# The store of one expert as four DMAs of 112, 10, 5 and 1 rows

## The chip, the cores and the metric

The kernel runs on one core of a Trainium2 chip. The metric is the device time of one execution in microseconds (us), as the median of several runs. One execution was also recorded by the hardware profiler; the lines shown in this document come from its trace.

Of the core's engines, TensorE (PE, and PEld for its weight loads) multiplies, VectorE (DVE) and ScalarE (ACT) move results out of PSUM and transpose, GpSimd (POOL) issues the loads of the weights, and SyncE (SP) issues the stores and hands out releases. The core has 16 DMA engines, which all queues share. A DMA that has landed adds 16 to its semaphore, one for each of these engines.

## The reference

Eight experts, each a two-layer network on its own 256 rows, in float32:

```python
n_experts, capacity, hidden, expert_hidden = 8, 256, 512, 2048
h = np.matmul(x, w1) + b1[:, np.newaxis, :]
h = np.maximum(h, 0)
return (np.matmul(h, w2) + b2[:, np.newaxis, :]).astype(np.float32)
```

The weights are 4 MB each for w1 and w2 of one expert, 64 MB together. The output is 8 x 256 x 512 float32, 4 MB, or 512 KB for one expert.

## The kernel before

The work is laid out in steps `s`. In step `s` TensorE computes the first layer of expert `s` and then the second layer of expert `s - 3` (LAG = 3). So the last three steps have a second layer alone: experts 5, 6 and 7. The first layer is 16 column blocks of 128 with four matmuls each; ScalarE adds the bias, applies relu and writes float16. The second layer has two row blocks `tb` of 128 rows and 16 contractions `j` each. It runs in a loop of two turns of 14 matmuls, and four matmuls behind them. Before each of the two turns TensorE waits for one release (`s_go`), which it takes off the semaphore at the turn's end.

Weights come in order on POOL's queue, converted to float16 on the way: w1 of the later experts, then w2. The w2 of the last two experts are cut, so that their parts can be released one by one: expert 6 in two halves, expert 7 in a half and two quarters.

When a second layer is done, ScalarE evicts the first row block from PSUM and VectorE the second (the copies at line 196). Results of experts 0 to 3 gather in one tile and of experts 4 and 5 in another; those of 6 and 7 have a tile each.

SP's program is one list, written out by hand (lines 249 to 276). For each step it waits for the weights (line 236) and gives the release (line 237). For the last step it reads:

```python
go(f"w2_{e}_0")
nc.sync.wait_ge(landed[f"w2_{e}_{second}"], 16)
for first in GROUPS:
    flush(first)
for tb in range(nTB):
    nc.sync.wait_ge(s_out[tb], e)
store(E - 2, 0, P, nc.sync)
go(f"w2_{e}_{third}")
```

The order is thus: the release for the first turn of expert 7; the stores of experts 0 to 3 (2 MB) and of 4 and 5 (1 MB), issued at line 241, as soon as the second part of w2 of expert 7 is there; the wait for the eviction of expert 6 (line 271); the store of expert 6 (line 247); the release for the second turn of expert 7, once the last quarter of its weights has landed. Behind that stand the waits for the eviction of expert 7 (line 275) and its store (line 247 again). SP executes this list strictly in order: what stands behind an instruction that takes long, waits with it.

In the 128-row store of one expert, a row is one SBUF partition: two rows of the output, 4 KB. In the two gathered stores a partition has 16 KB and 8 KB.

All stores add to one semaphore, `s_last`. At the start it is raised by 16 for each store and lowered again behind the waits for the first data; an instruction of ScalarE at the kernel's end waits for 16 times the number of stores. For that the code counts the stores: `STORES = len(LATE) + len(GROUPS)`, which is 4.

Of the kernel before, what the change touches and what calls it, by code (L numbers as in the profile page):

```python
# [10 lines left out]
def kernel(  # L11
# [12 lines left out]
    nc = tc.nc  # L24
# [4 lines left out]
    E, T, H = x.shape  # L29
    M = w1.shape[2]  # L30
    P = 128
# [8 lines left out]
    NW = 3  # L40
    NPH = 4
    GROUPS = {0: 4, 4: 2}
    LATE = (E - 2, E - 1)
    CUTS = {E - 2: (0, half, nJ), E - 1: (0, half, half + half // 2, nJ)}
    X_LOADS = {2: 2, 4: 4}
    group_of = {first + i: (first, n) for first, n in GROUPS.items() for i in range(n)}
# [5 lines left out]
    def sem(name):  # L52
        return ctx.enter_context(nc.semaphore(name=name))
# [45 lines left out]


    s_last = sem("last_stores")
    STORES = len(LATE) + len(GROUPS)
    nc.vector.sem_inc(s_last, 16 * STORES)


# [71 lines left out]
    tc.wait_critical_data_deps()  # L177
    nc.vector.sem_inc(s_last, -16 * STORES)
    nc.vector.sem_inc(s_xT, 1)
# [55 lines left out]
    def go(key, n=1):  # L235
        nc.sync.wait_ge(landed[key], 16)  # L236
        nc.sync.sem_inc(s_go, n)  # L237

    def flush(first):
        n = GROUPS[first]  # L240
        nc.sync.dma_start(
            out=out[first : first + n].rearrange("e (p r) h -> (e p) r h", r=n * nTB),
            in_=results[first][:]).then_inc(s_last, 16)

    def store(e, p0, p1, engine):
        dst = out[e].rearrange("(p r) h -> p r h", r=nTB)
        engine.dma_start(out=dst[p0:p1], in_=results[e][p0:p1]).then_inc(s_last, 16)

    for s in range(E + LAG):
        if s == 0:  # L250
            nc.sync.wait_ge(landed["b2"], 16)
        if s < E:
            nc.sync.wait_ge(s_xT, s + 1)
            go(f"w1_{s}")
        e = s - LAG
        if e >= 2:
            for tb in range(nTB):
                nc.sync.wait_ge(s_out[tb], e - 1)
        if e >= 0 and e not in CUTS:
            go(f"w2_{e}_0", 2)  # L260
        elif e == E - 2:
            go(f"w2_{e}_0")
            go(f"w2_{e}_{half}")
        elif e == E - 1:
            _, second, third, _ = CUTS[e]
# [3 lines that stand above are left out]
                flush(first)  # L269
            for tb in range(nTB):  # L270
                nc.sync.wait_ge(s_out[tb], e)
            store(E - 2, 0, P, nc.sync)
            go(f"w2_{e}_{third}")
    for tb in range(nTB):
        nc.sync.wait_ge(s_out[tb], E)
# [62 lines left out]
    section.close()  # L338
    landing = nc.scalar.nop().wait_op(s_last, 16 * STORES, "sem-ge")
    tc.add_manual_dep(landing.ins, by_hand.name, mybir.DependencyInfo(  # L340
# [31 lines left out]
```

## Time and profile before

| What | us |
|---|---|
| median of the runs (180.67 to 180.83) | 180.68 |
| the profiled execution | 180.71 |
| its span, first to last instruction | 178.9 |
| TensorE busy | 134.0 |
| ScalarE busy | 75.6 |
| VectorE busy | 65.0 |
| POOL busy | 12.4 |

The mean granted clock of TensorE is 0.976 of the full one. The span is 1.8 us shorter than the execution, since the start and the end of the program lie around it. A row of the timeline gives start, duration, engine, line, operation and what it writes and reads; in brackets stands the idle time of the engine before it and what ended that. `SPq` is an instruction that SP's sequencer carries out, such as issuing a DMA: its duration is the time in which SP can do nothing else, and has nothing to do with how long the data take. The time "to landing" goes from the start of the issue to the last of its 16 counts.

### The profile page before, as it was taken

What the parts mean: (1) busy time and instruction counts of PE and PEld (TensorE: products, weight loads), DVE (VectorE), ACT (ScalarE), POOL (GpSimd) and SP (SyncE); (2) the same over time, 40 slices, a digit from 0 to 9 for tenths busy, and PEclk for the clock granted to TensorE, in tenths of its full rate; (3) what the DMA queues carried; (4) which work ended last, traced back from release to release, by engine and by line L of the source; (5) the groups of instructions that cost most, each with busy time, mean ns of one, the idle gap of its engine ahead of it and who ended that gap; (6) DMA issues with size and microseconds to landing.
All of it is one profiled execution on the core that took longest, in us unless ns stands there. A gap on an engine that the chain in (4) does not pass through costs nothing. (4 is left out here: it accounts for less than half of the span.)

```text
span 178.9 us, 2980 instructions
## 1 busy us (share of the span) xinstructions
PE 134.0 (75%) x784; PEld 93.0 (52%) x784; DVE 65.0 (36%) x92; ACT 75.6 (42%) x153; POOL 12.4 (7%) x26
## 2 busy tenths in 40 slices
PE   0003978868699890998968896989698896999960
PEld 0003878858689330894458543874298442433420
DVE  1989928475000289600097006910330003031010
ACT  3201786757777113582087505680387201021010
POOL 4300012020200101001010001000200003000000
PEclk9999999999999999699999999699999999999997
DMA  6999999999998999999999999899999999999996
GB/s 218 266 205 207 234 205 205 234 216 196 236 223 185 236 227 194 223 231 201 212 234 209 201 234 223 190 231 231 194 220 231 205 209 211 216 216 207 355 414 256
DMA packets 3970, 40.46 MB, mean 226 GB/s; under 512 B 464, under 2 KB 480, under 8 KB 1408
## 3 DMA queue, kind: packets, MB, share of 16 engines
q0 software_dynamic: 3056, 35.14, 92.7%
q1 hardware_dynamic: 864, 5.24, 7.2%
q10 hardware_dynamic: 48, 0.07, 0.1%
q14 instruction: 2, 0.02, 0.0%
HBM read 71.39 MB, written 4.19 MB: 422 GB/s over the span
## 5 line engine op out<-in xcount | busy, mean ns | idle before, releaser
L297 PE MATMUL ph<-xT,w_sb 128*128 x512 | 72.5, 303 | 33.0 <-PEq L282 30.5
L297 PEld LDWEIGHTS ph<-xT,w_sb 128*128 x512 | 66.6, 146 | 39.9 <-issue 31.4
L224 ACT ACTIVATE hT<-ph,b1T 128x256 f16<-128x256 f32 x128 | 60.2, 475 | 33.4 <-PE ph L297 29.9
L314 PE MATMUL po<-w_sb,hT 128*128 x256 | 56.7, 379 | 2.2 <-issue 2.2
L120 DVE STREAM_TRANSPOSE xT<-x 32x256 f16<-32x256 f16 (+2 forms) x64 | 45.0, 702 | 27.3 <-DMA x<-in_x_dram 22.7
L314 PEld LDWEIGHTS po<-w_sb,hT 128*128 x256 | 24.9, 97 | 33.0 <-issue 7.0
L196 DVE COPY out<-po 32x512 f32<-32x512 f32 (+1 forms) x20 | 13.7, 687 | 63.1 <-PE po L314 62.9
L196 ACT COPY out<-po 32x512 f32<-32x512 f32 (+1 forms) x20 | 11.6, 578 | 46.0 <-PE po L314 45.8
L89 POOL DMA_DIRECT2D w_sb<-in_w_dram x19 | 10.7, 567 | 136.9 <-PE po L314 71.7
L324 PE MATMUL po<-b_sb,ones 1*128 x16 | 4.8, 378 | 3.9 <-issue 2.5
L196 ACT COPY x<-po 128x512 f32<-128x512 f32 x2 | 1.2, 586 | 14.2 <-PE po L314 14.2
L196 DVE COPY x<-po 128x512 f32<-128x512 f32 x2 | 1.4, 692 | 13.9 <-PE po L314 13.9
L324 PEld LDWEIGHTS po<-b_sb,ones 1*128 1x128 f16 x16 | 1.4, 90 | 6.6 <-issue 6.3
L181 DVE STREAM_TRANSPOSE b1T<-b_rows 32x512 f32<-32x512 f32 x4 | 4.1, 1024 | 0.5 <-issue 0.5
L135 ACT CAST x<-x 128x1024 f16<-128x1024 f32 x1 | 1.0, 1046 | 3.2 <-DMA x<-in_x_dram 3.2
L133 DVE CAST x<-x 128x1024 f16<-128x1024 f32 x1 | 0.7, 694 | 2.9 <-DMA x<-in_x_dram 2.9
L127 ACT ACT_TABLE_LOAD x1 | 1.3, 1283 | 0.7 <-PEq L356 0.7
L89 POOL DMA_DIRECT2D x<-in_x_dram x2 | 1.1, 544 | 0.0
L89 POOL DMA_DIRECT2D b_sb<-in_b_dram x1 | 0.5, 509 | 0.0
L126 DVE MEMSET ones<- 1x128 f16 x1 | 0.2, 165 | 0.9 <-PEq L356 0.9
L127 ACT ACTIVATE warm<-ones 1x128 f16<-1x128 f16 x1 | 0.3, 308 | 0.0
L356 POOL MEMSET const-float32-0.0<- 128x1 f32 x1 | 0.1, 99 | 0.2 <-issue 0.2
(3 smaller groups left out, 0.3 us busy)
## 6 DMA issues: line engine op xcount, KB each, us to landing
w_sb<-in_w_dram POOLq DMA_DIRECT2D x14, 2048.0 KB, 41.1
w_sb<-in_w_dram POOLq DMA_DIRECT2D x3, 1024.0 KB, 25.0
out_dram<-out SPq DMA_DIRECT2D x1, 2048.0 KB, 7.3
x<-in_x_dram SPq DMA_DIRECT2D x2, 512.0 KB, 3.8
x<-in_x_dram POOLq DMA_DIRECT2D x1, 1024.0 KB, 34.3
w_sb<-in_w_dram POOLq DMA_DIRECT2D x2, 512.0 KB, 18.2
out_dram<-out SPq DMA_DIRECT2D x1, 1024.0 KB, 9.4
out_dram<-x SPq DMA_DIRECT2D x2, 512.0 KB, 7.2
```

Source lines behind the costliest of these rows:

```text
L89: engine.dma_start(**kw).then_inc(landed[key], 16)
L120: last = nc.vector.transpose(out=mine[b * B : (b + 1) * B].rearrange("p kc (r g i) -> p g r kc i", r=R, i=B)[:, g], in_=src[:, :, b * (H / ...
L126: nc.vector.memset(ones1[:], 1.0)
L127: tc.keep_in_program_order(nc.scalar.activation(out=warm[:], in_=ones1[:], func=relu).then_inc(s_first, 1))
L133: nc.vector.tensor_copy(out=x16[0][0][:], in_=x32[0][:])
L135: tc.keep_in_program_order(nc.scalar.copy(out=x16[1][0][:], in_=x32[1][:]))
L181: turned = nc.vector.transpose(out=b1T[b * B : (b + 1) * B, nB - 1 - b : nB - 1 - b + nJ * B], in_=b1_rows[:].rearrange("r (i j) -> r j i" ...
L196: last = copy(out=results[e][at : at + rows, tb * n + k, :], in_=po[k * rows : (k + 1) * rows, bank : bank + H])
L224: nc.scalar.activation(out=dst, in_=src, func=relu, bias=b1T[:, bias_at : bias_at + 1], scale=1.0,).then_inc(s_credit, 1)
L297: last = nc.tensor.matmul(ph[:, j % NPH, 0:T], w1_sb[:, bass.ds(w_from + (kc * M + j), P, nJ)], xT[:, bass.ds(x_at + kc * T, T)], start=(k ...
L314: return nc.tensor.matmul(banks[tb], hT[:, bass.ds(h_from + (j * nTB + tb) * P, P)], w2_sb[:, bass.ds(w2_from + j * H, H)], start=False, s ...
L324: nc.tensor.matmul(banks[tb], ones1[:], b2_sb[:, bass.ds(s * H, H)], start=True, stop=False)
```

## The change

The store of expert 6, one DMA of 128 partitions, becomes four DMAs of 112, 10, 5 and 1 partitions. They stand at the same place of SP's list, behind the wait for the eviction of expert 6 and ahead of the release for the second turn of expert 7. The bytes are the same. The number of stores that the last wait counts rises from 4 to 7 (`len(DEAL)` is 5: four parts of expert 6 and the store of expert 7).

```diff
     GROUPS = {0: 4, 4: 2}
-    LATE = (E - 2, E - 1)
...
-    STORES = len(LATE) + len(GROUPS)
+    DEAL = (0, 112, 122, 127, 128)
+    STORES = len(GROUPS) + len(DEAL)
...
             for tb in range(nTB):
                 nc.sync.wait_ge(s_out[tb], e)
-            store(E - 2, 0, P, nc.sync)
+            for p0, p1 in zip(DEAL, DEAL[1:]):
+                store(E - 2, p0, p1, nc.sync)
             go(f"w2_{e}_{third}")
```

## The prediction

> **What bounds the kernel now.** I read the page's slices and chain first, then the DMA queues, then the last 15 us.
>
> ```profile
> span 178.9 us, 2980 instructions
> ...
> GB/s 218 266 205 207 234 205 205 234 216 196 236 223 185 236 227 194 223 231 201 212 234 209 201 234 223 190 231 231 194 220 231 205 209 211 216 216 207 355 414 256
> ...
> q0 software_dynamic: 3056, 35.14, 92.7%
> q1 hardware_dynamic: 864, 5.24, 7.2%
> ...
> DMA 22%; PE 22%; issue 2%; DVE 0%; ACT 0%; SPq 0%
> ...
> out_dram<-out SPq DMA_DIRECT2D x1, 2048.0 KB, 7.3
> ...
> out_dram<-out SPq DMA_DIRECT2D x1, 1024.0 KB, 9.4
> out_dram<-x SPq DMA_DIRECT2D x2, 512.0 KB, 7.2
> ```
>
> The weight loads on queue q0 fill the 16 DMA engines until about 166 us; in the last slices SP's queue q1 drains all 4 MB of output. The whole change lies in this tail. The busy time in stretches of it (columns: stretch, its length, then PE, PEld, DVE, ACT, POOL; granted clock, DMA share, GB/s):
>
> ```profile
> 166.00:168.00 2.00, 2.00 (x10) 0.97 (x10) 0.00 (x0) 0.00 (x0) 0.00 (x0) 1.00 1.13 311
> 168.00:170.00 2.00, 2.00 (x10) 0.87 (x9) 0.00 (x0) 0.00 (x0) 0.00 (x0) 1.00 1.01 434
> 170.00:172.00 2.00, 2.00 (x11) 0.89 (x10) 0.00 (x0) 0.00 (x0) 0.00 (x0) 1.00 1.01 434
> 172.00:174.00 2.00, 1.01 (x5) 0.27 (x3) 0.69 (x1) 0.59 (x1) 0.00 (x0) 1.00 0.92 389
> 174.00:176.00 2.00, 0.00 (x0) 0.00 (x0) 0.00 (x0) 0.00 (x0) 0.00 (x0) 1.00 0.98 406
> ```
>
> From 168 us the engines store at 434 GB/s, 27.1 GB/s each, without a gap. TensorE finishes at 173.0, DMA only at the end. The timeline of SP, TensorE and VectorE, start and duration in us:
>
> ```profile
> 157.88 7.08 PE L314 MATMUL po<-w_sb,hT 128*128 x32 [0.26 <-issue]
> 165.76 0.82 SPq L241 DMA_DIRECT2D out_dram<-out  x2
> 165.88 7.13 PE L314 MATMUL po<-w_sb,hT 128*128 x32 [0.30 <-issue]
> 166.69 1.74 SPq L247 DMA_DIRECT2D out_dram<-x  x1
> 168.94 0.10 PEld L314 LDWEIGHTS po<-w_sb,hT 128*128 x1 [0.37 <-issue]
> 173.04 0.69 DVE L196 COPY x<-po 128x512 f32<-128x512 f32 x1 [7.36 <-PE po L314]
> 173.83 0.33 SPq L247 DMA_DIRECT2D out_dram<-x  x1
> ```
>
> The reader is to see that the 512 KB store of expert 6 holds SP 1.74 us, and that the second half of expert 7's matmuls sits behind it: SP's next instruction is the release for that half, at 168.5 (the last start in the L237 row below). TensorE just feels it: the weight load at 168.94 has a gap of 0.37 us.
>
> ```profile
> L237 SPq EVENT_SEMAPHORE  x18: 17/28/9606, 15.4 to 168.5; - x18
> ...
> L241 SPq DMA_DIRECT2D out_dram<-out x2: 348/387/426, 165.8 to 166.2; - x2
> L247 SPq DMA_DIRECT2D out_dram<-x x2: 333/1036/1740, 166.7 to 173.8; - x2
> ...
> DMA to landing us min/median/max: 4.2/8.4/10.1
> ```
>
> So the last store, issued at 173.83, lands 4.2 us later, 178.03. From there to the end of the span are 0.87 us. The profiled execution's own time is 180.71, 1.81 over its span and 0.03 over the median of the runs, 180.68.
>
> **Why the issue takes 1.74 us.** Four issues of stores have the same form; three took 333, 348 and 426 ns. What was different? Packets that began in a stretch, by queue:
>
> ```profile
> q0 software_dynamic: 79, 0.32, 104.7%
> issues: line engine op xcount, KB each, median us to landing
> out_dram<-out SPq DMA_DIRECT2D x1, 2048.0 KB, 7.3
> out_dram<-out SPq DMA_DIRECT2D x1, 1024.0 KB, 9.4
> out_dram<-x SPq DMA_DIRECT2D x1, 512.0 KB, 10.1
> ...
> q1 hardware_dynamic: 16, 0.26, 100.6%
> q0 software_dynamic: 22, 0.03, 26.2%
> ```
>
> The first five lines are 165.76 to 167.27: all three stores are issued, yet only weights move. The last two are 167.27 to 167.89: 16 packets of q1, 16 KB each, the first row of the 2 MB store on each of the 16 engines. The held issue ends at 166.69 + 1.74 = 168.43, 0.54 after the slowest engine turned to q1. When the last store is issued at 173.83, the 2 MB store has landed (165.76 + 7.3 = 173.1) and the 1 MB store is under way, and the issue takes 333 ns. Both fit one reading: two stores of this queue may stand that have not begun on every engine, and a third issue holds SP until the older of the two has begun everywhere. That is inferred from one hold.
>
> **The change, part by part.** Removed: one issue of 128 rows. Added: issues of 112, 10, 5 and 1 rows in its place, same waits ahead, same bytes, and three more counted completions. Behind them on SP stand the release for the second half of expert 7, the waits for its eviction, and the last store. POOL's queue issues nothing more by then.
>
> (1) *112 rows.* It meets the same two stores ahead: 1.74 us, until 168.43. No change.
>
> (2) *10 rows.* Lower bound, an unhindered issue, 0.33 us. Upper: until the 1 MB store has begun everywhere. The 2 MB ahead of it take 2.097 MB / 434 GB/s = 4.83 us from 167.89, so 172.72, and with the lag of 0.54 the issue ends at 173.26. I take the upper one: its nearest row is the 1740 ns one, with two unbegun stores ahead as here, not the 333 ns one.
>
> (3) *5 rows.* Lower bound 0.33 again. Upper: until the 112 rows have begun: 1.049 MB / 434 = 2.42 us more, 175.14, and 0.54: 175.68. Taken for the same reason.
>
> (4) *1 row.* Between 0.33 and the 1.06 us that 112 rows take (0.459 MB / 434) with the lag of 0.54 once more. I take 0.39, the mean of the two unhindered issues at L241, since the ten rows stand on fewer engines: 176.07. The release follows at 176.1 instead of 168.5: 7.6 us later. TensorE has nothing else: its queue goes on only after that release, so all 7.6 reach the last matmul, 173.02 + 7.6 = 180.6.
>
> (5) *The clock.* A TensorE that stood idle came back at half clock:
>
> ```profile
> 71.84 3.36 PE L297 MATMUL ph<-xT,w_sb 128*128 x17 [4.95 <-PEq L282]
> ```
>
> ```profile
> 88.25:91.66 3.41, 1.88 (x10) 0.91 (x8) 1.90 (x3) 2.31 (x4) 0.53 (x1) 1.00 1.09 231
> 91.66:95.07 3.41, 3.41 (x28) 3.34 (x28) 3.34 (x5) 2.78 (x6) 0.00 (x0) 1.00 1.06 226
> 108.73:112.14 3.41, 1.79 (x14) 1.52 (x12) 3.07 (x5) 2.81 (x6) 0.53 (x1) 1.00 1.09 231
> 112.14:115.55 3.41, 3.41 (x19) 2.70 (x18) 3.38 (x3) 2.14 (x5) 0.00 (x0) 0.50 1.03 221
> 67.77:71.18 3.41, 0.00 (x0) 0.00 (x0) 3.34 (x5) 1.06 (x2) 0.00 (x0) 1.00 1.09 231
> 71.18:74.59 3.41, 2.75 (x13) 2.21 (x14) 3.38 (x3) 0.95 (x2) 0.00 (x0) 0.50 1.08 231
> ```
>
> After a stretch with 1.79 us of matmuls the next ran at 0.50; after 1.88 us it ran at full clock. After 7.6 us of idling a trip is near certain. Bounds: 0 and, for a whole 3.41 us at half clock, 1.7. I take 1.4, half of the 2.75 us that the last row shows after the longest idle time: 182.0. The Trainium skill, "TensorE: Matmul & The Clock Gate", Part 1 on the HAM clock gate, calls the window free-running; by that the penalty depends on where the resumption falls, and the term would be any value between these bounds. The rows here cannot show its phase in another run.
>
> (6) *Eviction and last store.* 173.83 - 173.02 = 0.81 us as before: issue at 182.8. By then everything else has drained, so it lands sooner than in 4.2 us. Bounds: 1.2 (0.524 MB / 434 GB/s) and 4.2. The nearest row is x's load of the same size, issued by SP on idle engines:
>
> ```profile
> L131 SPq DMA_DIRECT2D x<-in_x_dram x2: 383/405/427, 0.7 to 1.2; - x2
> ...
> DMA to landing us min/median/max: 3.2/3.8/4.3
> ```
>
> I take its least, 3.2: landed at 186.0. Sum: 186.0 + 0.87 + 1.81 = 188.7.
>
> (7) *How the rows spread.* Stores before went in 16 equal shares (the 16 first rows above); no row shows another split. A row of 4 KB is 0.15 us of one engine. If the small pieces give the first engines up to three rows more and the last one fewer, the drain moves by -0.15 to +0.45 us; all 16 rows on one engine would be 2.4. Taken as 0, since in this forecast the drain is long over when the last store begins.
>
> **Rivals.**
>
> *A, not slower: the hold is a single one.* Once q0 is empty, SP may be free. For it: three of four issues took 333 to 426 ns, and the hold ended as the last weights ended. Against it: 348 and 426 ns were had while q0 was still full. Then each added issue costs 0.39 and some 0.05 between: 1.3 us, release at 169.8, last matmul 174.3, last store issued 175.1. On idle engines that lands at 178.3 by the 3.2; the queue ahead lets it land at 178.0 at the earliest. The cover is this drain: 178.03 - 3.2 = 174.8 is the point from which issuing later costs time. With (7) I put it at 178.1, in all 180.8. The Trainium skill, "DMA: Bandwidth & Descriptors", section on why a DMA increments its semaphore by 16, says that SP's DMA runs on the lowest-numbered k engines, k at most 16 and dividing the rows. By that, 112, 10 and 5 rows go on 16, 10 and 5 engines, the last six get 0.15 us less, and A would be 180.6 if one of these six lands last; no run here shows which engine does. That stays within 0.2%, 0.36 us, which I take as the bound below which a measurement of this kernel can't tell a difference.
>
> *B, a hold by rows waiting.* Each engine holds so many rows, and each piece adds a row and its closing mark, two steps of 16 KB / 27.1 GB/s = 0.60 us: 1.2 us a piece, release at 172.1, last matmul 176.6 and 178.0 with (5), last store issued at 178.8, landed 182.0: 184.7. For it: one step was passed when the held issue ended. Against it: that the count was short by just one then would be chance.
>
> *C, A with a clock trip.* TensorE's idle time of 1.3 + 0.2 us comes near the 1.62 us (3.41 - 1.79) that tripped it; 1.7 us more put the last store at 176.8 and its landing at 180.0: 182.7.
>
> **How the numbers follow.** Forecast 50%, 188.7, its own range 186.0 to 190.4 (down by the clock's 1.4 and by 1.3 of the landing, up by 0.3 and 1.0 of the same two and by 0.4 for a longer hold of the single row). B 15%, C 4%, A 27%; a gain over 0.2% 4%, as (7) reaches only 0.15 us. So slower 0.69, same 0.27, faster 0.04. The range must reach A, and below its 180.8 by the 0.15 of (7) and as much again for what 3.2 may overstate: 180.4 to 190.4. Outside lie the 4% of a gain and about 10% for holds longer than the forecast's.
>
> **What would show it.** Right: issues at L247 of 1.7, some 4.8, some 2.4 us and a short one; the last start of L237 near 176; an idle time of over 7 us inside expert 7's matmuls; a half-clock stretch after it; GB/s falling to near nothing between 177 and 183. Wrong: four issues that sum to under 3.2 us and a last landing still near 178 (A), or issues of about 1.2 us (B). What would make it wrong is above all the inferred limit of two: if small stores need no such place, (2) and (3) vanish together.

## The result, and the profile after

The changed kernel takes 182.65 us (median of 17 runs, 181.81 to 184.35), the kernel before 180.76 (17 runs, 180.65 to 181.61). The ratio is 1.0116, with a 95% interval of 1.0096 to 1.0135: slower by 1.2%. The sign was forecast, the size was not: the forecast of 188.7 was 8.0 us over the kernel before, and 1.9 us were lost. The profiled execution took 182.51.

The page after: the slices, and the chain that ended last, by engine and by line.

```profile
span 180.7 us, 2983 instructions
...
GB/s 204 275 210 198 232 228 185 225 232 214 196 232 201 219 218 232 221 189 228 232 218 189 232 228 203 207 232 228 181 228 232 221 187 221 210 209 213 425 396 122
...
DMA 22%; PE 20%; SPq 3%; issue 2%; DVE 1%; ACT 0%
DMA w_sb<-in_w_dram 22%; PE po L315 15%; PE ph L298 5%; SPq L247 3%; PE po L325 1%; DVE x L196 1%; ACT hT L224 0%; SPq L237 0%; SPq L271 0%; SPq L236 0%
```

New in the chain is SP with 3% of the span, on line 247, the issues of the pieces. The same chain in order of time (start, duration, what):

```profile
166.32 0.70 DVE x L196
167.02 0.02 issue
167.03 0.02 SPq L271
167.05 0.04 issue
167.09 1.20 SPq L247
168.30 0.06 issue
168.35 1.28 SPq L247
169.63 0.05 issue
169.68 1.06 SPq L247
170.75 0.04 issue
170.79 1.04 SPq L247
171.82 0.05 issue
171.88 0.02 SPq L237
171.90 0.46 issue
172.35 4.07 PE po L315 x18
```

The four issues take 1.20, 1.28, 1.06 and 1.04 us. The release stands at 171.88; before it was at 168.5. TensorE's view of this is one row of the waits (who waited, for whom, in all, times, longest):

```profile
PE po L315 <- SPq L237: 2.4, 1, 2.4
```

Its last matmul ends at 176.42, 3.4 us later than before (173.02), and the last store is issued at 177.22 in place of 173.83. The stretches of the tail show what of that was covered:

```profile
168.00:170.00 2.00, 1.94 (x9) 0.69 (x7) 0.00 (x0) 0.00 (x0) 0.00 (x0) 1.00 0.97 418
170.00:172.00 2.00, 0.00 (x0) 0.00 (x0) 0.00 (x0) 0.00 (x0) 0.00 (x0) 1.00 1.09 467
172.00:174.00 2.00, 1.65 (x8) 0.87 (x9) 0.00 (x0) 0.00 (x0) 0.00 (x0) 1.00 0.91 385
174.00:176.00 2.00, 2.00 (x11) 0.88 (x9) 0.00 (x0) 0.00 (x0) 0.00 (x0) 1.00 0.96 391
176.00:178.00 2.00, 0.41 (x2) 0.00 (x0) 0.69 (x1) 0.58 (x1) 0.00 (x0) 1.00 0.09 35
```

From 170 to 172 TensorE does nothing, and the DMA engines drain the stores as before. From 176 to 178 the drain has run dry (35 GB/s), and the last store is issued only at 177.22. It then lands in 2.6 us, at 179.8, where it took 4.2 before behind the others. So 3.4 us later, 1.6 us sooner: 1.8 us in the span, 180.7 against 178.9.

The limit that the forecast rested on is refuted by this trace alone. Packets of SP's queue that began between 165.8 and 172.24:

```profile
q1 hardware_dynamic: 128, 2.10, 76.1%
```

These are the 128 rows of the 2 MB store and nothing else. By then all six issues were over (the last ended at 171.82) while the 1 MB store had not begun a row. The second, third and fourth piece did not wait for any store to begin: between 168.35 and 171.82 none did.

### The profile page after: what moved, and what is told of

It is laid out like the page before. It is cut to its first block, busy times and chain, and to the rows that moved or that the text cites. A ratio compares the mean times of both kernels' runs of the same rounds, so it can differ in the third digit from the quotient of the medians.

```text
span 180.7 us, 2983 instructions
## 1 busy us (share of the span) xinstructions
PE 135.4 (75%) x784; PEld 93.1 (52%) x784; DVE 65.1 (36%) x92; ACT 75.5 (42%) x153; POOL 12.2 (7%) x26
## 5 line engine op out<-in xcount | busy, mean ns | idle before, releaser
L315 PE MATMUL po<-w_sb,hT 128*128 x256 | 58.5, 387 | 4.0 <-SPq L237 2.4
```

Source lines behind the costliest of these rows:

```text
L315: return nc.tensor.matmul(banks[tb], hT[:, bass.ds(h_from + (j * nTB + tb) * P, P)], w2_sb[:, bass.ds(w2_from + j * H, H)], start=False, s ...
```

## The experiments

The question was why an issue of a few rows holds SP for a microsecond, and whether that is all that the change costs. Theory F: a store that takes fewer than 16 DMA engines has a fixed price. Theory W: each engine has place for a limited number of rows, so a piece waits until its rows fit (the mechanism of rival B). Theory L: an issue passes its DMA on in the background, and an issue that follows closely waits for that.

**Four pieces of 32 rows**, all on 16 engines.

```diff
-    DEAL = (0, 112, 122, 127, 128)
+    DEAL = (0, 32, 64, 96, 128)
```

> The store of expert 6 as four DMAs of 32 rows each, so that every one can run on all 16 engines, two rows on each. Theory F, a fixed price: an issue of a store that takes fewer than 16 engines holds SP some 1.05 us by itself (1.28, 1.06 and 1.04 us in the changed kernel), and one on 16 engines does not. Then the first of the four takes up to 1.7 us, the other three 0.33 to 0.43 each, the release comes near 169.7 and the time is 180.5 to 181.2. Theory W, rows waiting: each engine has place for a limited number of rows, and each further store waits until its rows and its closing mark fit. Then each of the last three, with two rows and a mark in place of one and a mark, holds SP at least as long as in the changed kernel, 1.0 to 1.9 us, the release comes at 171.5 to 174 and the time is 182 to 185.

Measured: 182.9 us, ratio 1.0108 (1.0093 to 1.0122). The issues of its store line, and its release line (durations least, median, most; first and last start):

```profile
L247 SPq DMA_DIRECT2D out_dram<-x x5: 354/1211/1213, 166.8 to 178.5; - x5
```

```profile
L237 SPq EVENT_SEMAPHORE  x18: 17/28/9607, 15.7 to 171.5; - x18
```

The first piece took 0.85 us, the others 1.21 each, though all 16 engines share them. F falls: the small number of engines isn't what costs.

This trace also speaks against the limit of two for the first piece, which met the same two stores as in the kernel before. Its hold ended at 167.63. Packets of SP's queue that had begun by 167.64, 16 KB each:

```profile
q1 hardware_dynamic: 11, 0.18, 23.3%
```

The 2 MB store had not begun on every engine when SP was free; the 16 first rows had begun only by 168.0.

**The four pieces behind the release.**

```diff
+            go(f"w2_{e}_{third}")
             for p0, p1 in zip(DEAL, DEAL[1:]):
                 store(E - 2, p0, p1, nc.sync)
-            go(f"w2_{e}_{third}")
```

> The four stores of 112, 10, 5 and 1 rows as in the changed kernel, but behind the release for the second turn of expert 7. Both theories have TensorE unhindered: last matmul at 172.8 to 173.0, and the four issues done before the eviction of expert 7 at 173.7. If the lost time went through the release alone, the time is that of the kernel before or up to 0.15 us less (180.4 to 180.8). If the small stores also cost something in the drain of the DMA engines, it is over 181.0.

Measured: 181.58 us, ratio 1.0034 (1.0021 to 1.0047). TensorE ended at 173.01, as before, so the hold is off its path. By the ratio 0.6 us stay lost: this is the second branch of the expectation, over 181.0, so the late release is not all that the change costs. The first two issues of this kernel:

```profile
168.46 0.35 SPq L247 DMA_DIRECT2D out_dram<-x  x1
```

```profile
168.86 1.26 SPq L247 DMA_DIRECT2D out_dram<-x  x1
```

The 112 rows, issued 1.8 us after SP's last issue, take 0.35 us. The ten rows right behind them take 1.26.

**The pieces on an empty queue**: x of expert 0 loaded in the same four parts.

```diff
-        tc.keep_in_program_order(nc.sync.dma_start(
-            out=x32[e][:], in_=x[e].rearrange("(p tb) h -> p tb h", tb=nTB)))
+        for p0, p1 in zip(PARTS[e], PARTS[e][1:]):
+            tc.keep_in_program_order(nc.sync.dma_start(
+                out=x32[e][p0:p1], in_=x[e].rearrange("(p tb) h -> p tb h", tb=nTB)[p0:p1]))
```

> The kernel before, with the load of x of expert 0, SP's first DMA, as four loads of 112, 10, 5 and 1 rows. SP's queue is empty then. Theory F: the first issue takes 0.38 us, the other three 1.0 to 1.1 us each, and the load of expert 1 some 0.4 again. Theory W: nothing is waiting, so all five take 0.35 to 0.45 us. The time is of no interest here; the first transposes come later by what the issues take.

```profile
L133 SPq DMA_DIRECT2D x<-in_x_dram x5: 247/360/397, 0.7 to 2.2; - x5
```

Five loads, 0.25 to 0.40 us each. F falls once more: 10, 5 and 1 rows cost no more than 128 here. The one execution took 181.53 us.

**112, 8, 4 and 4 rows.**

```diff
-    DEAL = (0, 112, 122, 127, 128)
+    DEAL = (0, 112, 120, 124, 128)
```

> The store of expert 6 as four DMAs of 112, 8, 4 and 4 rows. Theory F: the last three take fewer than 16 engines, so each holds SP some 1.05 us, whether 8 or 4 rows, and the time is 181.8 to 182.7 as in the changed kernel. Theory W: 8, 4 and 4 rows put one row and a mark on each of their engines, so again 1.0 to 1.3 us each. The run tells whether the price goes with the number of engines left out: then 8 rows cost more than 10 did less hold, and 4 and 4 the same as each other.

```profile
L247 SPq DMA_DIRECT2D out_dram<-x x5: 364/1100/1657, 166.9 to 179.2; - x5
```

The first took 1.66, the pieces 1.31, 1.08 and 1.10 us, so the number of engines left out does not set the price. The release came at 172.2. The one execution took 184.46, more than expected, because TensorE's clock was halved behind its idle time: its last 18 matmuls took 5.67 us. The same is shown for another run further below.

**The whole store behind the release**, the control for the second run.

```diff
-            store(E - 2, 0, P, nc.sync)
             go(f"w2_{e}_{third}")
+            store(E - 2, 0, P, nc.sync)
```

> The kernel before, with its one store of 128 rows behind the release for the second turn in place of ahead of it. It is the control for the run with the four pieces behind the release, which came out 0.34% slower than the kernel before although its TensorE was not held. If the small stores themselves cost that in the drain, this kernel takes 180.6 to 180.9 us, the time of the kernel before. If the place behind the release costs it (the store of expert 6 is issued 1.8 us later), this kernel too takes 181.2 to 181.7.

Measured: 180.87 us, ratio 1.0001 (0.9991 to 1.0011). The 128 rows took 0.33 us at this place. So the place behind the release costs nothing, and what the second run lost came with the split.

**The pieces ahead of the large stores.**

```diff
-            for first in GROUPS:
-                flush(first)
             for tb in range(nTB):
                 nc.sync.wait_ge(s_out[tb], e)
             for p0, p1 in zip(DEAL, DEAL[1:]):
                 store(E - 2, p0, p1, nc.sync)
+            for first in GROUPS:
+                flush(first)
```

> The four stores of 112, 10, 5 and 1 rows ahead of the 2 MB and 1 MB stores, so that nothing of SP's queue waits ahead of them; the weight loads still fill the engines until 167.3. Theory W, rows waiting: the pieces have nothing ahead but one another, so each issue takes 0.25 to 0.45 us, and if anything is held it is the 1 MB store; release at 168.3 to 169.0, time 180.5 to 181.2. Theory L, one hand-over at a time: an issue that follows another closely waits some 1.0 to 1.3 us while the 16 engines are busy, whatever is queued: the last three pieces and both large stores are held, the release comes at 170.5 to 172.5 and the time is 182 to 185.

Measured: 181.43 us, ratio 1.0046 (1.0022 to 1.0071). The issues of the two large stores:

```profile
L241 SPq DMA_DIRECT2D out_dram<-out x2: 360/396/432, 167.9 to 168.3; - x2
```

Six issues back to back took 0.36, 0.40, 0.58, 0.39, 0.36 and 0.43 us, while weights and rows of 4 KB moved; the first row of 16 KB began at 168.76, when the last of the six was over. L in the form given falls: busy engines are not enough. The release came at 168.8, TensorE ended at 173.3. The time is a little over W's range.

**The 1 MB store ahead of the 2 MB store**, with pieces of 32 rows.

```diff
-    DEAL = (0, 112, 122, 127, 128)
+    DEAL = (0, 32, 64, 96, 128)
...
-            for first in GROUPS:
+            for first in reversed(GROUPS):
                 flush(first)
```

> The four stores of 32 rows as in the earlier run, but the 1 MB store is issued ahead of the 2 MB store, so that rows of 8 KB in place of 16 KB move while the pieces are issued. An engine took 0.31 us for a row of 8 KB and 0.61 for one of 16 KB. If the hold of 1.21 us a piece is two rows that have to leave, whether by theory W or as a hand-over behind two rows, the second and third piece take some 0.6 us each. If it is a fixed time while the engines are busy, they take 1.21 again.

```profile
L247 SPq DMA_DIRECT2D out_dram<-x x5: 354/1217/1487, 167.2 to 179.6; - x5
```

The second piece, from 168.74 to 169.94, took 1.21 us while rows of 8 KB left, not 0.6. The third, from 170.00, took 1.23, but the engines were turning to rows of 16 KB by then (between 169.88 and 170.6), so it says less. The hold is not the time that two rows need to leave. The one execution took 184.86: the release came at 172.5, and the last 18 matmuls ran in part at half clock (5.74 us).

**Two halves of 64 rows.**

```diff
-    DEAL = (0, 112, 122, 127, 128)
+    DEAL = (0, 64, 128)
```

> The store of expert 6 as two DMAs of 64 rows. Theory W: the second brings four rows and a mark to each engine in place of the two rows and a mark of the 32-row pieces, so its issue takes twice theirs, some 2.4 us. Theory L: the second issue takes 1.21 us as the 32-row pieces did, since the price goes by the issue and not by the rows. Release near 170.8 (W) or 169.6 (L).

```profile
168.27 1.32 SPq L247 DMA_DIRECT2D out_dram<-x  x1
```

The second half took 1.32 us where W asks for 2.4: the price goes by the issue, not by the rows. The release was at 169.6, and the one execution took 181.06, within what the kernel before varies (180.68 to 181.54 beside it). So the drain covered all or nearly all of a release that came 1.1 us late.

**Pieces with pauses between them**: 64, 32 and 32 rows behind the release, the last two at counts that TensorE gives.

```diff
-            for p0, p1 in zip(DEAL, DEAL[1:]):
-                store(E - 2, p0, p1, nc.sync)
             go(f"w2_{e}_{third}")
+            store(E - 2, 0, 64, nc.sync)
+            nc.sync.wait_ge(s_mark, 2 * nTB * (E - 1) + 3)
+            store(E - 2, 64, 96, nc.sync)
+            nc.sync.wait_ge(s_mark, 2 * nTB * E)
+            store(E - 2, 96, 128, nc.sync)
...
                     for j in range(TURN):
-                        second(tb, h_from, w2_from, j)
+                        last = second(tb, h_from, w2_from, j)
+                    last.then_inc(s_mark, 1)
```

> The release first, then the store of expert 6 as three DMAs of 64, 32 and 32 rows with pauses between them: TensorE counts up a semaphore every seven matmuls, and SP issues the second and the third store at such counts, near 170.6 and 172.2 us. The 2 MB and 1 MB stores are queued ahead as in the changed kernel. Theory L in its present form: an issue passes its DMA on in the background, which takes some 1.2 us when two large stores are queued, and only the next issue waits for it. Then all three issues take 0.25 to 0.45 us, although the queue is as deep as before. Theory W, the depth of the queue itself: each takes 0.9 to 1.3 us again.

The three issues:

```profile
168.59 0.53 SPq L248 DMA_DIRECT2D out_dram<-x  x1
```

```profile
171.66 0.35 SPq L248 DMA_DIRECT2D out_dram<-x  x1
```

```profile
173.17 0.32 SPq L248 DMA_DIRECT2D out_dram<-x  x1
```

With the same two stores ahead and pauses of 2.5 and 1.2 us, nothing is held. How closely an issue follows another decides here. Against W this run says less than was expected of it: at 0.61 us a row of 16 KB, four of them leave an engine in 2.5 us, so W's places come free in a pause as well. What W cannot explain are the halves (1.32 in place of 2.4 us) and the rows of 8 KB (1.21 in place of 0.6). The one execution took 181.21 us.

**One large store ahead**: only the 2 MB store, with the 1 MB store behind the release.

```diff
-    DEAL = (0, 112, 122, 127, 128)
+    DEAL = (0, 32, 64, 96, 128)
...
-            for first in GROUPS:
-                flush(first)
+            flush(0)
...
             go(f"w2_{e}_{third}")
+            flush(4)
```

> Four stores of 32 rows back to back, with only the 2 MB store ahead of them; the 1 MB store is issued behind the release. If passing on is slow only with two large stores queued ahead, the four issues take 0.35 to 0.5 us each and the release comes near 168.5. If one large store that has not moved its rows is enough, the later pieces take 1.21 us each as with two, and the release comes at 169.5 to 171.

```profile
L247 SPq DMA_DIRECT2D out_dram<-x x5: 351/1202/1792, 167.2 to 177.5; - x5
```

The pieces (32 rows each) took 0.36, 1.37, 1.20 and 1.79 us: one large store is enough. The release, at 172.2, was later than expected, since the last piece was held longest. Why, is open. The one execution took 182.79 us.

**Even pieces behind the release.**

```diff
-    DEAL = (0, 112, 122, 127, 128)
+    DEAL = (0, 32, 64, 96, 128)
...
+            go(f"w2_{e}_{third}")
             for p0, p1 in zip(DEAL, DEAL[1:]):
                 store(E - 2, p0, p1, nc.sync)
-            go(f"w2_{e}_{third}")
```

> Four stores of 32 rows each, two rows on every engine, behind the release. With 112, 10, 5 and 1 rows at this place the time was 0.34% over the kernel before, and with one store of 128 the same as before. If the uneven share of rows costs that (ten rows of expert 6 on one engine, seven on others), this kernel takes the time of the kernel before, 180.6 to 181.0. If four DMAs in place of one cost it, whatever their share, it takes 181.2 to 181.7.

Measured: 181.78 us, ratio 1.0056 (1.0041 to 1.0071). Two rows of every piece on every engine cost no less than the uneven share. So it is four DMAs in place of one, not the share. In the traces, 256 rows of 4 KB belong to the last two stores. In the kernel before, the control, the run on the empty queue and the one with the late release, no such row took over 176 ns. In every kernel with a split store some took over 200: 2 in the changed kernel, 13 with its pieces behind the release (up to 0.52 us for a single one), 20 here (up to 0.46). Slow rows go with the split; why a piece's rows are sometimes slow, and how much of the lost time they make, is not shown.

**ScalarE issues the pieces**, on its own queue.

```diff
-            for p0, p1 in zip(DEAL, DEAL[1:]):
-                store(E - 2, p0, p1, nc.sync)
...
+        if s == E + LAG - 1:
+            nc.scalar.wait_ge(s_out[0], E - 1)
+            nc.scalar.wait_ge(s_out[1], E - 1)
+            for p0, p1 in zip(DEAL, DEAL[1:]):
+                store(E - 2, p0, p1, nc.scalar)
```

> The four stores of 112, 10, 5 and 1 rows issued by ScalarE, on its own queue, in which nothing else waits, while the 2 MB and 1 MB stores stand in SP's queue. If the hold belongs to the queue with the large stores ahead, ScalarE's four issues take 0.25 to 0.5 us each. If it belongs to the DMA engines or to a part that both queues share, the last three take 1.0 to 1.3 us each there too. SP's release is not behind them, so the time is 180.5 to 181.5 either way.

```profile
L216 ACTq DMA_DIRECT2D out_dram<-x x4: 337/1062/1658, 167.3 to 170.3; - x4
```

0.34, 1.66, 0.92 and 1.21 us in a queue in which nothing stood but these pieces. The hold does not come from the large stores' place in the same queue. The one execution took 181.84, over the 180.5 to 181.5 expected: here rows of 16 KB were slow too, up to 1.15 us for one.

**The late release alone**: one whole store, no added DMA. ScalarE makes ten copies into a spare tile, and SP waits for them ahead of the release.

```diff
+    s_spin = sem("spin")
+    spare = sbuf("spare", [P, 10 * 504], fp16)
...
+        if s == E + LAG - 1:
+            nc.scalar.wait_ge(s_out[1], E - 1)
+            for i in range(10):
+                spin = nc.scalar.copy(out=spare[:, i * 504 : (i + 1) * 504], in_=b1T[:, 4:508])
+            spin.then_inc(s_spin, 1)
...
             store(E - 2, 0, P, nc.sync)
+            nc.sync.wait_ge(s_spin, 1)
             go(f"w2_{e}_{third}")
```

> The kernel before with its one store of 128 rows. The release for the second turn is held back without any added DMA: ScalarE, which is idle then, makes ten copies into a tile of its own after the eviction of expert 6, and SP waits for the last of them. Ten copies of some 0.5 us from 165.7 put the release near 171 to 172, where it is in the changed kernel (171.9). If the late release alone costs what the change costs, the time is 181.8 to 183, with single executions up to 184.5 where TensorE's clock is halved after its idle time. If the pieces themselves cost a good part, it is at most 181.3.

Measured: 183.6 us, ratio 1.016 (1.0135 to 1.0185), over the 181.8 to 183 expected, with a release at 172.3, 0.4 us later than in the changed kernel:

```profile
L244 SPq EVENT_SEMAPHORE  x18: 17/28/9607, 15.4 to 172.3; - x18
```

```profile
172.83 4.06 PE L322 MATMUL po<-w_sb,hT 128*128 x18 [2.84 <-SPq L244]
```

A late release without one added DMA costs as much as the change and more: 0.46 us in the profiled executions (182.97 against 182.51), where the release is 0.4 us later. It is enough by itself.

**The last store in pieces.** The store of expert 6 is whole and behind the release.

```diff
-    store(E - 1, 0, P, nc.sync)
+    for p0, p1 in zip(DEAL, DEAL[1:]):
+        store(E - 1, p0, p1, nc.sync)
```

> The store of expert 6 whole and behind the release, and the last store, of expert 7, as four DMAs of 32 rows. They are issued from 174.0 on, while the last rows of 8 KB leave (until some 175.1) and rows of 4 KB follow. If the hold needs the large rows, the first issue takes 0.35 us, the second is held until about 175.2, and the third and fourth take 0.35 to 0.6 again. If it comes with any issue that follows another closely, the last three take 1.2 us each, the last is issued at 177.3 and the time is 1 to 2 us over the kernel before.

The last store's four issues:

```profile
173.79 0.34 SPq L248 DMA_DIRECT2D out_dram<-x  x1
```

```profile
174.19 0.72 SPq L248 DMA_DIRECT2D out_dram<-x  x1
```

```profile
174.96 0.45 SPq L248 DMA_DIRECT2D out_dram<-x  x1
```

```profile
175.45 0.57 SPq L248 DMA_DIRECT2D out_dram<-x  x1
```

As the form with large rows had it: only the second is held, until 174.91, about when the last row of 8 KB begins (174.93), and behind it the issues are short. The one execution took 180.76, the time of the kernel before.

**The clock behind the idle time.** In the run with 32-row pieces TensorE came back like this:

```profile
171.94 5.74 PE L315 MATMUL po<-w_sb,hT 128*128 x18 [2.78 <-SPq L237]
```

```profile
172.57:175.98 3.41, 3.41 (x9) 1.21 (x8) 0.00 (x0) 0.00 (x0) 0.00 (x0) 0.50 1.00 407
```

18 matmuls took 5.74 us in place of the 4.07 above: 1.7 us for 3.41 us at half clock. In the profiled execution of the changed kernel the clock stayed whole there, although the idle times, 2.41 and 2.78 us, differ little. What differed is how they fell on stretches of 3.41 us. In the kernel before, the half clock began at 71.18 and at 112.14, twelve such steps apart, and each time lasted one. Counted in these steps from a half-clock stretch of each trace (from 150.96 in the changed kernel, from 172.57 in the run with 32-row pieces), the stretches that hold the idle time are, the changed kernel first:

```profile
168.03:171.44 3.41, 1.91 (x9) 0.69 (x7) 0.00 (x0) 0.00 (x0) 0.00 (x0) 1.00 1.04 447
171.44:174.85 3.41, 2.50 (x12) 1.27 (x13) 0.00 (x0) 0.00 (x0) 0.00 (x0) 1.00 0.94 395
```

```profile
169.15:172.56 3.41, 0.63 (x4) 0.38 (x4) 0.00 (x0) 0.00 (x0) 0.00 (x0) 1.00 0.97 416
```

In the changed kernel the idle time was split between two stretches, which kept 1.91 and 2.50 us of matmuls; in the run with 32-row pieces it lay in one, which kept 0.63. The other executions of the changed kernel took up to 184.35, which a halved clock in a part of them would give; without their traces that is not shown.

## Why the prediction was wrong, step by step

**The failed step: the hold of the second and third piece, (2) and (3).** They were priced with the rule that two stores may stand unbegun and a third issue holds SP until the older has begun on every engine: 4.8 and 2.4 us. They took 1.28 and 1.06. The rule had been read from one hold of 1.74 us, and it fitted that hold and the short issue at 173.83. Of the 6.2 us by which 188.7 exceeds the profiled execution, 4.2 are this release, 1.4 the clock and 0.6 the landing.

The runs show another rule in its place. An issue that started within 0.5 us of the end of another on the same issuing engine, and ran at least in part while the large stores' rows left (from 167.3 on in the kernel before), took 0.85 to 1.8 us, mostly 1.0 to 1.3, whatever its own size, its engines or its queue. Near the end of these rows three such issues took 0.72, 0.45 and 0.49. After a pause of 0.95 us or more, or where it was over before these rows began, an issue took 0.25 to 0.6. That a large store stands ahead is not enough: the 1 MB store, issued 0.05 us behind the 2 MB store before a row of either had begun, took 0.43. The hold of the kernel before fits this too: the same 128 rows took 0.33 us when issued after a pause of 1.8 us.

Of the issues held on SP, those behind a piece on 16 engines took 1.19 to 1.79 us, and those behind one of 10 rows or fewer 1.04 to 1.10 (the three near the end left out). That fits theory L, in which an issue waits until the one ahead is passed on, but no run was made to test it. What in the chip takes this time is open.

(1) *112 rows*: 1.20 us in place of 1.74; it ended at 168.30, so the end of the hold was right within 0.13. That is no support for the rule: the first piece of 32 rows was free at 167.63, before the 2 MB store had begun everywhere. In the profiled execution expert 6 was evicted later (167.0), since TensorE ran at half clock for 3.4 us from 151 on; that hardly moved the release, which waited for SP.

(4) *1 row*: taken at 0.39, measured 1.04. This went the other way: the row was said to be nearly free. The release came 3.4 us late, not 7.6. That all of it reaches the last matmul was right: 3.4 there too.

(5) *The clock*: the size was about right (1.7 us in the run above, 1.4 taken), but a halving was near certain only for an idle time of 7.6 us. With 2.4 us it hung on how that time fell on the stretches, and in the profiled execution it cost nothing.

(6) *The last store*: lands 2.6 us after its issue on idle engines, where the load of x had suggested 3.2.

(7) *The share of the rows*: the uneven share was there. The semaphore of the stores has 83 updates in the trace: 16 each for the two gathered stores, the last store and the 112 rows, then 10, 5 and 1 for the small pieces, and three single ones, each 0.1 to 0.2 us behind the end of a small piece's issue (169.75, 170.91 and 171.99), that make up for the engines left out. The rule on k of the Trainium skill, "DMA: Bandwidth & Descriptors", section on why a DMA increments its semaphore by 16, agrees with these counts. The cost of the uneven share was put at nothing, within a bound of 0.45 us that counted one row too many: seven rows of the first piece and three more are two over the eight of one store, 0.30. Behind the release the pieces cost 0.34%, together with slow rows that the working did not have, and an even share did no better.

**The rivals.** A is wrong in its hold, but its cover was real: the point from which a later last store costs time was put at 174.8, and the half-stores, with theirs at 174.98, took 181.06, hardly over the kernel before. With 2.6 in place of 3.2 the point is 178.0 - 2.6 = 175.4. (A's own 3.2 would have landed its last store at 178.3 and not at the 178.1 that it summed.) B had 1.2 us a piece and the release at 172.1; measured 171.88. Its size was thus right to the release, by a mechanism that the halves and the rows of 8 KB refute, so that this was luck; its 184.7 came out too high by the clock (1.4) and the landing (0.6). C's 182.7 lies by the median too, again by luck: its issues were to be short, and they were not.

## What to carry to other kernels

The price of an added DMA is also what its issue holds up behind it in the same list: look at what stands next in the queue's program, and put releases that others wait for ahead of stores that nobody waits for. Here the release ahead of the pieces took the hold off TensorE's path; for the one whole store, whose hold ended just in time, the order made no difference (ratio 1.0001). One held issue in a trace gives no rule for how long the next is held; price such a step by a range from the short issue to the held one, and not by a mechanism that has been seen once. And a drain at the end covers lateness only up to a point: compute it (end of the drain less the time of one unhindered store) and compare with what the change delays.

## What the runs showed of the hardware

In one execution, issues on ScalarE's own queue were held like those on SP's (up to 1.66 us), although the large stores stood in SP's queue. Closely following issues were short (0.36 to 0.58 us) while weight loads filled all 16 engines, and held (0.85 to 1.8 us) while rows of 16 or 8 KB of large stores left. A pause of 1.2 us between issues was enough to make them short beside these rows (0.32 us); one of 0.5 us was not (1.20 us). A store of 128 rows split into pieces had rows of 4 KB that took up to 0.52 us in place of 0.16, and cost 0.34 to 0.56% off TensorE's path. TensorE's clock was halved in the stretch after one with 0.63 or 1.79 us of matmuls in 3.41, and not after one with 1.88 or 1.91. In the run with the late release it was not halved after one with 1.76 either, so these rows give no firm bound:

```profile
171.18:174.59 3.41, 1.76 (x9) 0.90 (x10) 0.00 (x0) 1.14 (x3) 0.00 (x0) 1.00 0.97 411
174.59:178.00 3.41, 2.29 (x11) 0.86 (x9) 0.69 (x1) 0.59 (x1) 0.00 (x0) 1.00 0.45 185
```
